# Half of the 128-row chunks kept in reverse order, so that two chunks share one left operand in the level products of a recurrent (HGRN2) branch

## The chip, the cores and the metric

The kernel runs on one core of a Trainium2 chip. The metric is the device time of one execution in microseconds (us); the median of several runs is given. The core has a matrix engine (TensorE, PE; its loads of the left operand are shown apart as PEld), VectorE (DVE), ScalarE (ACT), GpSimd (POOL), and SyncE (SP), which here only issues DMAs. The engines run side by side and wait for one another through semaphores. On-chip memory has 128 partitions; TensorE writes to a separate accumulator memory, PSUM, of which the kernel uses eight banks of 128 x 512 fp32 in three rings (`pj` 3, `z` 2, `ms` 3).

## The reference

A decoder block in fp32 over 1024 rows of width 1024: a norm, one projection to nine parts, two branches side by side, a gated sum of both, an output projection with a residual, and a dense SwiGLU FFN.

```python
xn = rms_norm(x, norm1_g); proj = xn @ w_in
q_sb, k_sb, v_sb, q_hg, f_hg, i_hg, g_hg, gate_sb, gate_hg = split_cols(proj, IN_SIZES)
# attention branch, 8 heads of 64: strictly causal stick-breaking
z = q @ k.T * scale; causal = s_idx < t_idx
sp = where(causal, softplus(z), 0); rest = cumsum(sp, reverse=True) - sp
w = where(causal, exp(log_sigmoid(z) - rest), 0); o = w @ v
# HGRN2 branch, 4 heads of 128, in order of the rows t
f = lb + (1 - lb) * sigmoid(f_hg); key = 1 - f; q = silu(q_hg)
S_t = diag(f_t) @ S_{t-1} + key_t * i_t^T;  o_t = S_t^T @ q_t
o = rms_norm(o, norm_g) * silu(g_hg)
# merge and FFN
h = x + (sigmoid(gate_sb) * (o_sb @ Wb0) + sigmoid(gate_hg) * (o_hg @ Wb1)) @ w_out
out = h + (silu(hn @ w_gate) * (hn @ w_up)) @ w_down          # hn = rms_norm(h, norm2_g)
```

In the HGRN2 branch a chunk of rows is solved at once: with b the running sum of log f over the chunk, row t gets from row s <= t the weight sum over k of q[t,k] key[s,k] exp(b[t,k] - b[s,k]).

## The kernel before, in words

All tensors lie transposed: channels in the partitions, rows (time) along the free axis. The 1024 rows are two halves (`h`) of 512, a half is four chunks of 128 rows. The x tensor comes in once, is split into a high and a low fp32r part, and stays on chip; each of the 44 column tiles of the input projection is 2 x 24 fp32r matmuls (`proj`, names `pj<-ah,oh`, `pj<-al,oh`, `pj<-ah,ol`).

The first part of the kernel (until about 700 us) holds the projections, the attention (`scores`, `values`) and the recurrent branch (`hgrn`). Operations aren't issued in program order: `Plan` collects them with their buffers and a guessed duration (`us`), and `issue()` lists them per engine: it steps through a guessed time and gives each engine the ready operation of the highest rank and, among those, of the longest remaining path. The order on each engine is thus fixed when the kernel is built, and it changes when a guessed duration changes. The projections have rank -1: TensorE takes them where nothing else is ready. Their own order is fixed by `FILL` (q, k, v as `a`, the HGRN2 parts `f`, `i`, `q`, `g`, the branch gates `G`). When the last operation of the first part is done, the pools are closed, the outputs of both branches, which were stored in DRAM (`o_d`), are loaded again (`ld`) and split (`o`), and the products with `w_branch` begin (`pj<-o,..`, `z<-o,..`).

The change lies around `hgrn`. For each head `hd` and half `h` it computes `key`, the running sums `bb` (one scan a chunk), and the 128 x 128 weights `at` of each chunk (keys in the partitions, queries along the free axis). The diagonal is a column sum (`sums`). The rest is done by levels m = 64, 32, ..., 1: in blocks of 2m rows, queries of the late half meet keys of the early half, and both are scaled against the running sum at the border, so that no exponent is positive:

- two differences on VectorE into `dl` (early keys, late queries), one Exp on ScalarE over the 512 columns, a product with `q` into `ql` and a product with `key` in `dl`;
- a matmul per chunk into `lv`: left operand `dl` of the chunk, without its last m columns, moving operand the 64 late queries of the chunk;
- the result goes to `at`, at m = 64 by a copy, below by a predicated copy with a mask of the level (`level_masks`, built on GpSimd and spread by VectorE at the start).

At m = 1 a column sum takes the place of the matmul. After the levels come the decays to the end of the chunk (`kd`, `bl`), the chunk states (`state`), the output and its norm and gate. `take` moves a projection out of PSUM: for q and k through `qk_in`, for v into `vx`. In `scores` the tile on the diagonal is masked with `future`. `setup` makes the constants. `sums`, `V`, `A`, `M`, `G` all record at one helper, so most rows of the profile have line 194 and are told apart by tile names.

Of the kernel before, what the change touches and what calls it, by code (L numbers as in the profile page):

```python
# [12 lines left out]
I8 = mybir.dt.int8  # L13
# [24 lines left out]


class View:  # L40

# [13 lines left out]
    def bitcast(self, d):  # L55
        return self._then(lambda t: t.bitcast(d))

    def to_broadcast(self, s):
# [156 lines left out]
def hybrid_block(ctx: ExitStack, tc, xT, wi, wb, wo, wg, wu, wd, vec, outT):  # L215
# [49 lines left out]
    bones_r = const1.tile([P, P], F32R, name="bones_r")  # L265
    future = const1.tile([P, P], I8, name="future")
    never = const1.tile([P, P], F32, name="never")
# [11 lines left out]
    def setup(sp):  # L279
        make_identity(nc, ident)  # L280
        t2 = sp.tile([P, P], F32, tag="t2", name="t2")
        nc.vector.memset(t2, 0.0)
        nc.vector.memset(t2[0:64, 0:64], 1.0)
        nc.vector.memset(t2[64:128, 64:128], 1.0)
        nc.vector.tensor_copy(bones_r, t2)
        nc.vector.memset(never, NEG)
        nc.gpsimd.memset(future, 1.0)
        nc.gpsimd.affine_select(
            out=future, in_=future, pattern=[[1, P]], compare_op=ALU.is_ge, fill=0.0,
            base=0, channel_multiplier=-1)  # L290
# [19 lines left out]
    def hs(h):  # L310
        return slice(h * HALF, (h + 1) * HALF)
# [56 lines left out]
    future = future.bitcast(U8)  # L368

# [9 lines left out]
        att: dict(aa=10, th=2, tl=2, ww=7, ot=2, pvt=1),  # L379
        hgp: dict(xf=2, xq=2, xi=2, xg=2, kb=4, dl=2, tail=4, ql=2,  # L380
                  state=5, bl=2),
# [111 lines left out]
    def level_masks():  # L493
        for m in LEVELS[1:]:
            mk = const1.tile([P, 4, 64], I8, name=f"mk{m}")
            one = new("tmp").bitcast(I8)[:, :64].rearrange("p (n m) -> p n m", m=m)
            G(nc.gpsimd.memset, one, 1.0, us=0.1, after=(last_split[0],))
            G(nc.gpsimd.affine_select, out=one, in_=one, pattern=[[-2 * m, 64 // m], [0, m]],
              compare_op=ALU.is_ge, fill=0.0, base=0, channel_multiplier=1, us=0.4)
            G(nc.gpsimd.affine_select, out=one, in_=one, pattern=[[2 * m, 64 // m], [0, m]],  # L500
              compare_op=ALU.is_ge, fill=0.0, base=m - 1, channel_multiplier=-1, us=0.4)
            mask = fixed(mk)
            V(nc.vector.tensor_copy, mask,
              one.rearrange("p n m -> p (n m)").rearrange("p (o t) -> p o t", o=1)
              .to_broadcast([P, 4, 64]), n=128)
            lvl_mask.append(mask.bitcast(U8))

# [79 lines left out]

    def qk_in(ps, g, h):
        x, sq = new("aa"), new("aa")
        V(tt, x, ps, rr[h], op=ALU.mult)  # L590
# [14 lines left out]
    def take(nm, u, h, ps):  # L605

        d = heads[u] if nm != "G" else None
        if nm in ("q", "k"):
            x = qk_in(ps, gains[nm], h)
            for e in range(2):  # L610
# [117 lines left out]
    def hgrn(hd, last):  # L728
# [3 lines left out]
        cs = [slice(c * P, (c + 1) * P) for c in range(4)]  # L732
        chunk = lambda t: t.rearrange("p (c t) -> p c t", t=P)
        for h in range(2):
# [4 lines left out]
            for c in cs:  # L739
                V(nc.vector.tensor_tensor_scan, bb[:, c], lf[:, c], lf[:, c], 0.0, op0=ALU.add,  # L740
                  op1=ALU.min, n=P)
            pair = lambda t, m: t.rearrange("p (n u m) -> p n u m", u=2, m=m)
            V(tt, at, key, q, op=ALU.mult, after=(last,))
# [4 lines left out]
            for li, m in enumerate(LEVELS):  # L748
                nb = HALF // (2 * m)
                bv = pair(bb, m)  # L750
                if m == 1:
                    e1 = new("ql", (P, HALF // 2))
                    ev = e1.rearrange("p (n m) -> p n m", m=1)
                    V(tt, ev, bv[:, :, 1, :], bv[:, :, 0, :], op=ALU.subtract, n=256)
                    A(act, e1, e1, AF.Exp, n=256)
                    for t, u in ((key, 0), (q, 1)):
                        V(tt, ev, ev, pair(t, 1)[:, :, u, :], op=ALU.mult, n=256)
                    lv = new("ms")
                    last = sums(lv[:, :256], e1, ones_r, 256, (last,))
                    V(nc.vector.copy_predicated, pair(at, 1)[:, :, 1, :],  # L760
                      lvl_mask[li - 1].rearrange("p c (n m) -> p (c n) m", m=1),
                      lv[:, :256].rearrange("p (n m) -> p n m", m=1), n=256)
                    continue
                rb = bv[:, :, 0, m - 1:m].to_broadcast([P, nb, m])
                dl, ql = new("dl"), new("ql", (P, HALF // 2))
                dv = pair(dl, m)
                V(tt, dv[:, :, 0, :], rb, bv[:, :, 0, :], op=ALU.subtract, n=256)
                V(tt, dv[:, :, 1, :], bv[:, :, 1, :], rb, op=ALU.subtract, n=256, part=True)
                A(act, dl, dl, AF.Exp)
                V(tt, ql.rearrange("p (n m) -> p n m", m=m), pair(q, m)[:, :, 1, :], dv[:, :, 1, :],  # L770
                  op=ALU.mult, n=256)
                V(tt, dv[:, :, 0, :], dv[:, :, 0, :], pair(key, m)[:, :, 0, :], op=ALU.mult, n=256)
                lv = new("ms")
                n = P - m
                last = M(0, [(lv[:n, c * 64:(c + 1) * 64], dl[:, c * P:c * P + n],
                                         ql[:, c * 64:(c + 1) * 64], True, True)
                                        for c in range(4)], after=(last,),
                         us=0.43 + 0.003 * n)
                dst, src = pair(at, m)[:n, :, 1, :], lv[:n, :256].rearrange("p (n m) -> p n m", m=m)
                if m == 64:  # L780
                    V(nc.vector.tensor_copy, dst, src, n=256)
                else:
                    V(nc.vector.copy_predicated, dst,
                      lvl_mask[li - 1][:n].rearrange("p c (n m) -> p (c n) m", m=m), src, n=256)
            kd, ktok, qe, bl = new("tail"), new("tail"), new("tail"), new("bl", (P, 4))
            b3 = chunk(bb)
            V(tt, chunk(kd), b3[:, :, P - 1:P].to_broadcast([P, 4, P]), b3, op=ALU.subtract,
              holds=(ktok, qe, bl))
            A(act, kd, kd, AF.Exp)
# [5 lines left out]
            d["free hq", h] = V(tt, qe, qe, q, op=ALU.mult)  # L795
            A(act, bl, b3[:, :, P - 1], AF.Exp, n=4)
            ds_ = new("ms")
# [389 lines left out]


def _layout(inputs):
    import numpy as np  # L1190

    def tiles(w):
# [12 lines left out]
    return {  # L1205
        "xT": np.ascontiguousarray(g["x"][0].T).reshape(KT, P, S),
        "wi": tiles(g["w_in"]), "wb": tiles(g["w_branch"]), "wo": tiles(g["w_out"]),
# [27 lines left out]
```

## Time and profile before

| | us |
|---|---|
| median of 3 runs (1519.15 to 1520.98) | 1520.84 |
| the profiled execution | 1520.8 |
| its span, first to last instruction | 1519.1 |
| busy: PE / DVE / ACT / POOL | 1501.8 / 1194.1 / 804.3 / 110.3 |
| level products on PE, 6 x 64 records: busy by the profile | 5.4, 6.7, 7.4, 7.7, 7.9, 8.0 |

A row such as `312.55 0.96 PE L194 MATMUL ms<-ql,dl 128*120 128x64 f32 x8` of the timeline says: at 312.55 us, lasting 0.96 us, TensorE, line 194, output `ms` from moving operand `ql` and left operand `dl`, left operand 128 partitions by 120 columns, 128 x 64 read, eight records. An fp32 matmul is two records, one of fp32r is one. In the list of groups, `x8 | 5.8, 723 | 2.1 <-PE ms` is count, busy us, mean ns of one, idle us ahead of them and what ended it. In the table of stretches each engine has its busy us and its count, then come the granted TensorE clock, the DMA share and GB/s. The ends of matmul records are modelled, and successive ones overlap.

### The profile page before, as it was taken

Reading aid. Unit: us, or ns where it says so; the run is one execution under the profiler, and the core shown is the slowest. Engines: PE = TensorE matmul, PEld = TensorE weight load, DVE = VectorE, ACT = ScalarE, POOL = GpSimd, SP = SyncE. Lnnn points to the kernel's source line nnn. Section 1 sums busy time; section 2 is a strip of 40 time slices with the busy share of each in tenths; the row PEclk is TensorE's granted clock in tenths of the full one; section 3 lists DMA queues with packets and bytes.
Section 4 is the critical chain, followed back from the end, with each engine's and each line's share of the span. In section 5 each row is a group of like instructions: output and inputs, shape, how many; then the busy total and the mean of one; then the engine's idle time right before and its main releaser. Section 6 shows DMA issues by size and latency. Waiting matters only on the chain.

```text
span 1519.1 us, 20504 instructions
## 1 busy us (share of the span) xinstructions
PE 1501.8 (99%) x7213; PEld 1238.3 (82%) x7213; DVE 1194.1 (79%) x2092; ACT 804.3 (53%) x1505; POOL 110.3 (7%) x155
## 2 busy tenths in 40 slices
PE   9999999999999999999999999999999999999999
PEld 6778888888888888888888888777888887888887
DVE  9898789988997877967867798788888888675553
ACT  7867779668758877445434453332332332354442
POOL 4210111211101100110000000000000000000000
PEclk9999999999999999999999999999999999999999
DMA  5111111111111212136434345444445544797662
GB/s 182 40 44 60 54 39 46 44 39 56 51 51 39 68 61 63 51 120 220 163 114 145 112 148 184 150 154 153 163 166 164 161 160 166 256 327 243 199 216 91
DMA packets 83159, 188.53 MB, mean 124 GB/s; under 512 B 9584, under 2 KB 11632, under 8 KB 83056
## 3 DMA queue, kind: packets, MB, share of 16 engines
q1 hardware_dynamic: 72400, 167.82, 34.2%
q10 hardware_dynamic: 10656, 19.40, 3.5%
q8 instruction: 57, 0.93, 0.3%
q14 instruction: 46, 0.38, 0.1%
HBM read 131.61 MB, written 55.57 MB: 123 GB/s over the span
## 4 chain that ended last, share of the span: by engine, by line
PE 69%; DVE 18%; DMA 5%; ACT 4%; issue 3%; POOL 1%; SPq 0%; DVEq 0%; ACTq 0%; POOLq 0%
PE pj L194 34%; PE f L1152 14%; PE ms L194 13%; PE z L194 8%; DVE ol L194 4%; DMA w<-wu 3%; DVE g L194 3%; DMA w<-wg 2%; DVE w L194 2%; DVE c L194 1%; DVE aa L194 1%; ACT aa L194 1%; ACT oh L194 1%; DVE kb L194 1%; DVE bs L194 1%
## 5 line engine op out<-in xcount | busy, mean ns | idle before, releaser
L194 PE MATMUL pj<-ah,oh 128*128 128x512 f32 x704 | 287.2, 408 | 2.4 <-ACT tmp L194 0.9
L194 PE MATMUL pj<-ah,ol 128*128 128x512 f32 x704 | 276.3, 393 | 0.0
L194 PE MATMUL pj<-al,oh 128*128 128x512 f32 x704 | 275.9, 392 | 0.0
L194 ACT CAST oh<-w 128x512 fp32r<-128x512 f32 x164 | 99.6, 619 | 237.3 <-DVE w L194 67.7
L194 DVE TENSOR_TENSOR ol<-w,oh 128x512 fp32r<-128x512 f32 x248 | 170.1, 686 | 31.0 <-ACT oh L194 23.5
L194 PE MATMUL ms<-f,oh 128*128 128x512 f32 x528 | 165.0, 394 | 3.1 <-DVE g L194 2.9
L194 PEld LDWEIGHTS pj<-ah,ol 128*128 128x128 f32 x704 | 132.6, 188 | 29.8
L194 PEld LDWEIGHTS pj<-ah,oh 128*128 128x128 f32 x704 | 132.9, 189 | 26.7 <-DVE aa L194 1.4
L194 PEld LDWEIGHTS pj<-al,oh 128*128 128x128 f32 x704 | 133.1, 189 | 23.1 <-DVE al L194 0.5
L194 PEld LDWEIGHTS ms<-f,oh 128*128 128x128 f32 x528 | 97.5, 188 | 29.5 <-DVE g L194 7.2
L1152 PE MATMUL f<-bh,ah 128*128 128x512 f32 x296 | 115.2, 389 | 0.0
L1152 PE MATMUL f<-bh,al 128*128 128x512 f32 x296 | 115.2, 389 | 0.0
L1152 PE MATMUL f<-bl,ah 128*128 128x512 f32 x296 | 115.1, 389 | 0.0
L194 DVE TENSOR_TENSOR_SCAN aa<-aa,ww 128x512 f32<-128x512 f32 (+3 forms) x96 | 94.2, 996 | 25.3 <-ACT aa L194 14.6
L194 PE MATMUL z<-f,oh 128*128 128x512 f32 x352 | 108.6, 390 | 0.0
L194 PE MATMUL pj<-f,oh 128*128 128x512 f32 x352 | 108.4, 389 | 0.0
L248 DVE TENSOR_TENSOR al<-ra,ah 128x512 fp32r<-128x512 f32 x73 | 50.4, 690 | 70.1 <-ACT ah L247 69.9
L194 PE MATMUL ms<-f,ol 128*128 128x512 f32 x264 | 102.9, 390 | 0.0
L194 POOL TENSOR_SCALAR oh<-w 128x512 fp32r<-128x512 f32 x84 | 68.4, 815 | 437.8 <-PE pj L194 367.7
L247 ACT CAST ah<-ra 128x512 fp32r<-128x512 f32 x73 | 45.5, 624 | 95.6 <-PE f L1152 83.8
L194 PE MATMUL pj<-mx,oh 128*128 128x512 f32 x256 | 78.7, 389 | 0.0
L194 PEld LDWEIGHTS pj<-f,oh 128*128 128x128 f32 x352 | 66.1, 188 | 13.7
(257 smaller groups left out, 3148.7 us busy)
## 6 DMA issues: line engine op xcount, KB each, us to landing
w<-wi SPq DMA_DIRECT2D x42, 512.0 KB, 3.6
rb<-act_d SPq DMA_DIRECT2D x73, 256.0 KB, 4.3
w<-wg SPq DMA_DIRECT2D x22, 512.0 KB, 4.3
w<-wu SPq DMA_DIRECT2D x22, 512.0 KB, 4.5
w<-wd SPq DMA_DIRECT2D x22, 512.0 KB, 5.0
wd_d<-ds SPq DMA_DIRECT2D x44, 256.0 KB, 2.8
ra<-wd_d SPq DMA_DIRECT2D x44, 256.0 KB, 4.1
act_d<-c SPq DMA_DIRECT2D x40, 256.0 KB, 4.2
```

The lines of the kernel that those rows point to most:

```text
L194: fn(*[a.real() if isinstance(a, View) else a for a in args], **{k: v.real() if isinstance(v, View) else v for k, v in kw.items()})
L247: pin(nc.scalar.copy(hi, src))
L248: pin(nc.vector.tensor_tensor(lo, src, hi.bitcast(F32), op=ALU.subtract))
L1152: nc.tensor.matmul(banks[SET[o]][d], l[:, ws], r, start=start and i == 0, stop=p == NP - 1 and i == 2, skip_group_check=True)
```

## The change

The rows of x are permuted on the host (`_order`): in each half, chunks 2 and 3 are kept in reverse order, chunks 0 and 1 in order. The output is put back on the host. Inside:

- `hgrn` scans the reversed chunks backwards. In a reversed chunk the early keys lie where a chunk in order has its late queries; `mixed` writes the early keys of chunk a (in order) and of chunk a + 2 (reversed) into one tile of 128 columns, interleaved by blocks of m. `packed` puts the late queries side by side into the second half of `dl` (the tile `ql` is gone). One matmul then has these 128 columns as left operand and 2 x 64 queries, of both chunks, as moving operand: two matmuls a level in place of four, with all 128 columns. Half of each result is meaningless and is left out by the mask.
- All levels, 64 too, now write with a predicated copy. There are seven masks, each with a form for either order, built over 128 columns and spread by four copies.
- Attention keeps queries in the stored order, and needs keys and values in true order: `ordered` takes k and v out of PSUM in two operations, the second one reversing its chunks. The diagonal mask has two forms.
- The planner's guess for a level product goes from 0.43 + 0.003 n (n = 128 - m) to 0.44 us.

```diff
@@ setup
-        nc.gpsimd.memset(future, 1.0)
-        nc.gpsimd.affine_select(out=future, ..., base=0, channel_multiplier=-1)
+        for f, base, step in ((future[0], 0, -1), (future[1], 1 - P, 1)):
+            nc.gpsimd.memset(f, 1.0)
+            nc.gpsimd.affine_select(out=f, in_=f, ..., base=base, channel_multiplier=step)
@@ level_masks
-        for m in LEVELS[1:]:
-            mk = const1.tile([P, 4, 64], I8, name=f"mk{m}")
-            one = new("tmp").bitcast(I8)[:, :64]...
+        for m in LEVELS:
+            mk = const1.tile([P, 2, 2, 64], I8, name=f"mk{m}")
+            one = new("tmp").bitcast(I8)[:, :P]...
...
-            V(nc.vector.tensor_copy, mask, one....to_broadcast([P, 4, 64]), n=128)
+            for e in range(2):
+                src = one.rearrange("p (n e) m -> p e n m", e=2)[:, e]
+                for a in range(2):
+                    V(nc.vector.tensor_copy, mask[:, e, a]..., src, n=64, part=True)
@@ qk_in (keys), take (v)
+    def ordered(x, ps, h):
+        V(tt, x[:, :256], ps[:, :256], rr[h][:, :256], op=ALU.mult, n=256, part=True)
+        chunk = lambda t: t.rearrange("p (a t) -> p a t", t=P)
+        V(tt, chunk(x[:, 256:])[:, :, ::-1], chunk(ps[:, 256:]), chunk(rr[h][:, 256:]), op=ALU.mult,
+          n=256, part=True)
-            V(tt, d["v"][:, hs(h)], ps, rr[h], op=ALU.mult, part=True)
+            ordered(d["v"][:, hs(h)], ps, h)
@@ scores
-                        V(nc.vector.copy_predicated, z[:, w - P:w], future, never, n=P)
+                        V(nc.vector.copy_predicated, z[:, w - P:w], future[tb // 2 % 2], never, n=P)
@@ hgrn
+        early = lambda t, m: t.strided(0, (256 + m, 2), (2 * m, P // m), (1, m))
+        late = lambda t, m: t.strided(m, (256 - m, 2), (2 * m, P // m), (1, m))
+        edge = lambda t, m: t.strided(m - 1, (257, 2), (2 * m, P // m), (0, m))
+        mixed = lambda t, m: t.strided(0, (m, 2), (2 * m, P // m), (1, m))
+        packed = lambda t, m, k=0: t.strided(k, (P, 2), (m, P // m), (1, m))
...
+            for i, c in enumerate(cs):
+                to, lc = (t[:, c] if i < 2 else t[:, c][:, ::-1] for t in (bb, lf))
+                V(nc.vector.tensor_tensor_scan, to, lc, lc, 0.0, op0=ALU.add, op1=ALU.min, n=P)
...
-                V(tt, dv[:, :, 0, :], rb, bv[:, :, 0, :], op=ALU.subtract, n=256)
-                V(tt, dv[:, :, 1, :], bv[:, :, 1, :], rb, op=ALU.subtract, n=256, part=True)
+                    dk, dq, rb = mixed(dl, m), packed(dl, m, 256), edge(bb, m)
+                    V(tt, dk, rb, early(bb, m), op=ALU.subtract, n=256)
+                    V(tt, dq, late(bb, m), rb, op=ALU.subtract, n=256, part=True)
                 A(act, dl, dl, AF.Exp)
...
-                last = M(0, [(lv[:n, c * 64:(c + 1) * 64], dl[:, c * P:c * P + n],
-                              ql[:, c * 64:(c + 1) * 64], True, True) for c in range(4)],
-                         after=(last,), us=0.43 + 0.003 * n)
+                    cols = lambda t, k: t.strided(k, (P, 2), (1, 64))
+                    last = M(0, [(cols(lv, 64 * a), dl[:, a * P:a * P + P],
+                                  cols(dl, 256 + 64 * a), True, True) for a in range(2)],
+                             after=(last,), us=0.44)
...
+                V(nc.vector.copy_predicated, late(at, m), packed(lvl_mask[li], m), packed(lv, m),
+                  n=256)
@@ _layout, kernel (host)
+    o = np.arange(S).reshape(S // HALF, 4, P)
+    o[:, 2:] = o[:, 2:, ::-1].copy()
```

More of the change, by code (lines that the diff above doesn't have):

```diff
@@ L37, with strided @@
 V_W = 27
+def strided(t, offset, *dims):
+    t = t[:]
+    return bass.AP(t.tensor, t.offset + offset, [t.ap[0], *(list(d) for d in dims)])
 class View:
@@ L56, in bitcast, with strided @@
         return self._then(lambda t: t.bitcast(d))
+    def strided(self, offset, *dims):
+        return self._then(lambda t: strided(t, offset, *dims))
     def to_broadcast(self, s):
@@ L265, in hybrid_block @@
     bones_r = const1.tile([P, P], F32R, name="bones_r")
-    future = const1.tile([P, P], I8, name="future")
+    future = [const1.tile([P, P], I8, name=f"future{i}") for i in range(2)]
     never = const1.tile([P, P], F32, name="never")
@@ L286, in setup @@
         nc.vector.memset(never, NEG)
-        nc.gpsimd.memset(future, 1.0)
-        nc.gpsimd.affine_select(
-            out=future, in_=future, pattern=[[1, P]], compare_op=ALU.is_ge, fill=0.0,
-            base=0, channel_multiplier=-1)
+        for f, base, step in ((future[0], 0, -1), (future[1], 1 - P, 1)):
+            nc.gpsimd.memset(f, 1.0)
+            nc.gpsimd.affine_select(out=f, in_=f, pattern=[[1, P]], compare_op=ALU.is_ge, fill=0.0,
+                                    base=base, channel_multiplier=step)
         nc.vector.tensor_scalar(qg, vt[:, V_Q:V_Q + 1], 0.125, None, op0=ALU.mult)
@@ L366, in hybrid_block @@
                          stop=i == WARM - 1)
-    future = future.bitcast(U8)
+    future = [f.bitcast(U8) for f in future]
     plan = Plan()
@@ L379, in hybrid_block @@
         att: dict(aa=10, th=2, tl=2, ww=7, ot=2, pvt=1),
-        hgp: dict(xf=2, xq=2, xi=2, xg=2, kb=4, dl=2, tail=4, ql=2,
+        hgp: dict(xf=2, xq=2, xi=2, xg=2, kb=4, dl=2, tail=4,
                   state=5, bl=2),
@@ L493, in level_masks @@
     def level_masks():
-        for m in LEVELS[1:]:
-            mk = const1.tile([P, 4, 64], I8, name=f"mk{m}")
-            one = new("tmp").bitcast(I8)[:, :64].rearrange("p (n m) -> p n m", m=m)
+        for m in LEVELS:
+            mk = const1.tile([P, 2, 2, 64], I8, name=f"mk{m}")
+            one = new("tmp").bitcast(I8)[:, :P].rearrange("p (n m) -> p n m", m=m)
             G(nc.gpsimd.memset, one, 1.0, us=0.1, after=(last_split[0],))
-            G(nc.gpsimd.affine_select, out=one, in_=one, pattern=[[-2 * m, 64 // m], [0, m]],
+            G(nc.gpsimd.affine_select, out=one, in_=one, pattern=[[-m, P // m], [0, m]],
               compare_op=ALU.is_ge, fill=0.0, base=0, channel_multiplier=1, us=0.4)
-            G(nc.gpsimd.affine_select, out=one, in_=one, pattern=[[2 * m, 64 // m], [0, m]],
+            G(nc.gpsimd.affine_select, out=one, in_=one, pattern=[[m, P // m], [0, m]],
               compare_op=ALU.is_ge, fill=0.0, base=m - 1, channel_multiplier=-1, us=0.4)
             mask = fixed(mk)
[L503 to L506, printed above, removed]
+            for e in range(2):
+                src = one.rearrange("p (n e) m -> p e n m", e=2)[:, e]
+                for a in range(2):
+                    V(nc.vector.tensor_copy, mask[:, e, a].rearrange("p (n m) -> p n m", m=m), src,
+                      n=64, part=True)
+            lvl_mask.append(mask.bitcast(U8).rearrange("p e a t -> p (e a t)"))
     xh = [[fixed(xn[k][0]) for h in range(2)] for k in range(KT)]
@@ L586, in sums, with qk_in @@
         return M(2 * n, [(out, w, hi, True, False), (out, w, lo, False, True)], after=after)
-    def qk_in(ps, g, h):
+    def ordered(x, ps, h):
[3 more added lines that the diff above has]
+          n=256, part=True)
+    def qk_in(ps, g, h, keys):
         x, sq = new("aa"), new("aa")
-        V(tt, x, ps, rr[h], op=ALU.mult)
+        if keys:
+            ordered(x, ps, h)
+        else:
+            V(tt, x, ps, rr[h], op=ALU.mult)
         A(act, sq, x, AF.Square)
@@ L733, in hgrn @@
         chunk = lambda t: t.rearrange("p (c t) -> p c t", t=P)
+        early = lambda t, m: t.strided(0, (256 + m, 2), (2 * m, P // m), (1, m))
[3 more added lines that the diff above has]
+        packed = lambda t, m, k=0: t.strided(k, (P, 2), (m, P // m), (1, m))
+        four = lambda t: t.rearrange("p (e a t) -> p e a t", e=2, a=2)
         for h in range(2):
@@ L748, in hgrn @@
             for li, m in enumerate(LEVELS):
-                nb = HALF // (2 * m)
-                bv = pair(bb, m)
+                dl, lv = new("dl"), new("ms")
                 if m == 1:
[L752 to L763, printed above, removed]
@@ L772, in hgrn @@
-                V(tt, dv[:, :, 0, :], dv[:, :, 0, :], pair(key, m)[:, :, 0, :], op=ALU.mult, n=256)
-                lv = new("ms")
-                n = P - m
-                last = M(0, [(lv[:n, c * 64:(c + 1) * 64], dl[:, c * P:c * P + n],
[L776 to L779, printed above, removed]
@@ L780, in hgrn @@
-                if m == 64:
-                    V(nc.vector.tensor_copy, dst, src, n=256)
-                else:
-                    V(nc.vector.copy_predicated, dst,
-                      lvl_mask[li - 1][:n].rearrange("p c (n m) -> p (c n) m", m=m), src, n=256)
+                    ev = packed(dl, 1)
+                    V(tt, ev, late(bb, 1), early(bb, 1), op=ALU.subtract, n=256)
+                    A(act, dl[:, :256], dl[:, :256], AF.Exp, n=256)
+                    for t in (early(key, 1), late(q, 1)):
+                        V(tt, ev, ev, t, op=ALU.mult, n=256)
@@ new lines, in hgrn @@
+                    last = sums(lv[:, :256], dl[:, :256], ones_r, 256, (last,))
+                else:
+                    dk, dq, rb = mixed(dl, m), packed(dl, m, 256), edge(bb, m)
+                    V(tt, dk, rb, early(bb, m), op=ALU.subtract, n=256)
+                    V(tt, dq, late(bb, m), rb, op=ALU.subtract, n=256, part=True)
+                    A(act, dl, dl, AF.Exp)
+                    V(tt, dq, late(q, m), dq, op=ALU.mult, n=256)
+                    V(tt, dk, dk, early(key, m), op=ALU.mult, n=256)
+                    cols = lambda t, k: t.strided(k, (P, 2), (1, 64))
+                    last = M(0, [(cols(lv, 64 * a), dl[:, a * P:a * P + P],
+                                  cols(dl, 256 + 64 * a), True, True) for a in range(2)],
+                             after=(last,), us=0.44)
@@ L785, in hgrn @@
+                V(nc.vector.copy_predicated, late(at, m), packed(lvl_mask[li], m), packed(lv, m),
+                  n=256)
             kd, ktok, qe, bl = new("tail"), new("tail"), new("tail"), new("bl", (P, 4))
-            b3 = chunk(bb)
-            V(tt, chunk(kd), b3[:, :, P - 1:P].to_broadcast([P, 4, P]), b3, op=ALU.subtract,
-              holds=(ktok, qe, bl))
+            V(tt, four(kd), bb.strided(P - 1, (P + 1, 2), (P, 2), (0, P)), four(bb),
+              op=ALU.subtract, holds=(ktok, qe, bl))
@@ L795, in hgrn @@
             d["free hq", h] = V(tt, qe, qe, q, op=ALU.mult)
[L796 removed]
+            A(act, bl.rearrange("p (e a) -> p e a", a=2), bb.strided(P - 1, (P + 1, 2), (P, 2)),
+              AF.Exp, n=4)
             ds_ = new("ms")
@@ L1186, in hybrid_block, with _order @@
         finish(o, d)
+def _order():
+    import numpy as np
+    o = np.arange(S).reshape(S // HALF, 4, P)
+    o[:, 2:] = o[:, 2:, ::-1].copy()
+    return o.reshape(S)
 def _layout(inputs):
@@ L1232 @@
     r = run_bass_kernel_spmd(nc, [arrays], core_ids=[0])
-    out = np.asarray(r.results[0]["outT"]).reshape(D, S)
+    out = np.asarray(r.results[0]["outT"]).reshape(D, S)[:, _order()]
     return np.ascontiguousarray(out.T).reshape(1, S, D)
```

14 lines of the change are left out of this document (2 added, 12 removed).

## The prediction

> **What bounds the kernel now.** I read the page first (busy shares, the chain that ended last), then the busy time by stretches, then TensorE's timeline inside the stretches that the change touches. The first 700 us of the span hold the input projections, the attention and the recurrent (HGRN2) branch; all that is edited lies there.
>
> ```profile
> span 1519.1 us, 20504 instructions
> PE 1501.8 (99%) x7213; PEld 1238.3 (82%) x7213; DVE 1194.1 (79%) x2092; ACT 804.3 (53%) x1505; POOL 110.3 (7%) x155
> PE 69%; DVE 18%; DMA 5%; ACT 4%; issue 3%; POOL 1%; SPq 0%; DVEq 0%; ACTq 0%; POOLq 0%
> ```
>
> TensorE is busy 99% and carries 69% of the chain that ended last. The ends of its records are modelled, so I don't take busy for full; I price its work by the distance from one start to the next. VectorE is the runner-up. The stretches of the level products, and the whole part from 45 to 700 us (columns: PE, PEld, DVE, ACT, POOL busy):
>
> ```profile
> 45.00:700.00 655.00, 648.67 (x3513) 544.08 (x3512) 550.17 (x1041) 473.04 (x956) 90.12 (x116) 1.00 0.20 62
> 88.00:136.00 48.00, 46.69 (x274) 39.04 (x275) 45.12 (x103) 29.32 (x58) 5.19 (x6) 1.00 0.15 48
> 256.00:322.00 66.00, 64.01 (x370) 53.80 (x369) 61.13 (x133) 41.60 (x81) 13.84 (x15) 1.00 0.14 44
> 405.00:440.00 35.00, 34.16 (x197) 27.98 (x197) 34.40 (x80) 16.84 (x32) 5.97 (x9) 1.00 0.19 63
> 614.00:660.00 46.00, 45.74 (x274) 38.72 (x273) 43.91 (x109) 19.22 (x35) 9.82 (x10) 1.00 0.19 59
> ```
>
> Over the whole part TensorE idles 6.3 us of 655 and VectorE 105 us. Inside the four level stretches (195 us) VectorE is busy 184.6, so it has only 10.4 us to spare there. TensorE never lacks work because the projections (rank -1, `pj<-ah,..`) fill each hole; a saving on TensorE therefore shortens the part as long as projections remain to be moved up.
>
> **The level products on TensorE (the gain).** Per half of a head there are six product groups, m = 64 to 2. Before, a group is four fp32 matmuls with 128-m left columns and 64 moving ones, and each fp32 matmul is two records: x8. After, it is two matmuls with 128 left and 128 moving columns: x4. One group of each width, with the start of what follows it:
>
> ```profile
> 643.47 0.68 PE L194 MATMUL ms<-ql,dl 128*64 128x64 f32 x8
> 644.07 0.50 PE L194 MATMUL pj<-ah,oh 128*128 128x512 f32 x1
> 644.88 0.81 PE L194 MATMUL ms<-ql,dl 128*96 128x64 f32 x8
> 645.50 0.47 PE L194 MATMUL pj<-ah,oh 128*128 128x512 f32 x1
> 648.81 0.95 PE L194 MATMUL ms<-ql,dl 128*112 128x64 f32 x8
> 649.59 1.11 PE L194 MATMUL ms<-xi,tail 128*128 128x128 f32 x8
> 312.55 0.96 PE L194 MATMUL ms<-ql,dl 128*120 128x64 f32 x8
> 313.31 0.47 PE L194 MATMUL ms<-th,bones_r 128*128 128x512 f32 x1
> 655.50 0.98 PE L194 MATMUL ms<-ql,dl 128*124 128x64 f32 x8
> 656.29 0.48 PE L194 MATMUL pj<-ah,oh 128*128 128x512 f32 x1
> 657.77 0.99 PE L194 MATMUL ms<-ql,dl 128*126 128x64 f32 x8
> 658.57 0.36 PE L194 MATMUL ms<-th,ones_r 128*128 128x256 f32 x1
> 306.38 0.60 PE L194 MATMUL ms<-ident,tail 128*128 128x128 f32 x4
> 306.74 0.48 PE L194 MATMUL pj<-ah,oh 128*128 128x512 f32 x1
> 654.16 0.39 PE L194 MATMUL ms<-tail,state 128*128 128x128 f32 x2
> 654.39 0.39 PE L194 MATMUL ms<-kb,xi 128*128 128x128 f32 x2
> ```
>
> The six groups take 0.60, 0.62, 0.78, 0.76, 0.79 and 0.80 us to the next start: 4.35 us per half. The moving columns are the same in all six, and yet the wide ones are a third longer: the loading of the left operand sets the pace. The new group is four records of 128 left and 128 moving columns. The nearest rows of that shape: four transposes, 0.36 us to the next start, and one fp32 matmul (two records) 654.16 to 654.39, 0.23 us. I take 0.37; 2 x 0.23 = 0.46 is the other end. Six groups: 2.22 us (2.76 at most). Eight halves: 8 x (4.35 - 2.22) = 17.0 us off TensorE (12.7 at least). The step of about 0.09 us that the first fp32r matmul behind a group costs (644.07 to 644.41 instead of 0.23) stays.
>
> [...]
>
> **VectorE.** Operation counts of a level stay: two differences, two products, one write of the result; they take half a tile each, as before. What is added:
>
> ```profile
> 667.71 0.68 DVE L194 TENSOR_TENSOR xg<-pj,rr 128x512 f32<-128x512 f32 x1
> 668.30 0.68 DVE L194 TENSOR_TENSOR ol<-w,oh 128x512 fp32r<-128x512 f32 x1
> 645.08 0.75 DVE L194 TENSOR_TENSOR dl<-kb 128x256 f32<-128x256 f32 x2
> 645.75 0.41 DVE L194 TENSOR_TENSOR ql<-kb 128x256 f32<-128x256 f32 x1
> L194 DVE COPY mk<-tmp 128x256 int8<-128x256 int8 x6 | 1.6, 283 | 0.6 <-POOL tmp L194 0.6
> L194 DVE COPY_PREDICATED kb<-mk,ms 126x256 f32<-126x256 uint8 x8 | 5.8, 723 | 2.1 <-PE ms L194 2.1
> L194 DVE COPY_PREDICATED kb<-mk,ms 96x256 f32<-96x256 uint8 x8 | 3.5, 437 | 0.0
> L194 DVE COPY kb<-ms 64x256 f32<-64x256 f32 x8 | 3.3, 408 | 0.0
> ```
>
> - k and v are taken out of PSUM in two pieces: 8 + 8 halves. One piece of 512 takes 0.59 us to the next start, two of 256 take 0.67: +0.08 x 16 = 1.3 us.
> - Masks: 6 copies of 256 bytes (1.6 us in all, 0.27 each) become 28 of 64 bytes. Between 0.07 (a quarter of that, nothing fixed) and 0.27 each: 1.9 to 7.6 us. I take 0.13, nearer the quarter, since 256 and 512 elements above (0.335 and 0.59 us) leave about 0.08 that doesn't shrink: 3.6, so +2.0 us, all in the first 45 us.
> - m = 64 becomes a predicated copy: 437 for 408 ns, x8, +0.2 us. Predicated copies at m = 2 and 1 keep their runs and their 0.72 us.
>
> Sum +3.5 us on an engine with 105 us free from 45 to 700 us. Ranges of the scan and of the last-column decay only change direction or step; I cost them at nothing, bounded by the same instruction counts.
>
> **GpSimd and start.** One more mask level, affine selects over 128 instead of 64 columns, a second causal mask:
>
> ```profile
> L194 POOL TENSOR_SCALAR_AFFINE_SELECT tmp<-tmp 128x64 int8<-128x64 int8 x12 | 7.6, 640 | 0.6
> 8.30 0.62 POOL L194 TENSOR_SCALAR oh<-kb 128x512 fp32r<-128x512 f32 x1 [4.47 <-DMA kb<-wi]
> 0.00:40.00 40.00, 36.94 (x137) 27.69 (x137) 36.37 (x71) 31.22 (x53) 16.63 (x34) 1.00 0.52 185
> ```
>
> The second causal mask (a fill and a select, 1.3 us at most by the row of the selects) comes ahead of a 4.47 us wait for a DMA: hidden. The selects of the levels: 14, each between 0.64 (the 64-wide row) and 1.28 us (twice that): 9.0 to 17.9 us against 7.6. I take 1.0: +6 us on an engine that is busy 16.6 of the first 40. The weight splits `oh` queue behind them, and VectorE's split behind those, then the projection. VectorE is busy 36.4 of those 40 us, so its +2.0 us and a late split are not fully covered: I charge 1.0 us, with 0 and 4 as ends (+2.0 and a delay of two selects).
>
> **What is late next.** In the level stretches TensorE loses 4.3 us of work per head; projections move up, and each brings VectorE about 1.2 us (an eviction, a weight split) per 5.45 us of matmuls (24 x 0.227): some 3.8 us into 10.4 us of room, but the third stretch has only 0.6. I charge 1.5 us. No DMA is moved past another: the order of loads and stores in SP's queue stays, each only earlier. The end of the part:
>
> ```profile
> 674.20 0.33 SPq L194 DMA_DIRECT2D o_d<-tail  x1
> 695.66 2.35 DVE L194 TENSOR_TENSOR o<-ld,o 128x1024 fp32r<-128x1024 f32 x2
> 700.49 0.62 PE L194 MATMUL pj<-o,oh 128*128 128x512 f32 x2
> 703.21 0.62 PE L194 MATMUL z<-o,oh 128*128 128x512 f32 x2
> ```
>
> The last store goes out at 674.2; the stored outputs come back and are split until 698.0; TensorE covers this with leftover gate projections until 700.5. The last split is wanted about 4.7 us after that start (its product is the last of the `z` group), so there are about 7 us of slack. If VectorE holds the last head's chain (614 to 660) at its length, 4.3 us of this go, and it still fits. Without that cover the overrun would be paid one to one.
>
> **Sum.** 17.0 - 1.0 - 1.5 = 14.5 us. The profiled execution took 1520.8 us around its span of 1519.1; the median of the runs is 1520.84, so the sum stands on both alike: 1506.3 us. From 700 us on nothing is edited.
>
> **Rivals.**
> - *VectorE takes the stretches.* The new patterns have one more step, and the differences and products of the left operand write interleaved. If an interleaved write cost what short runs cost the predicated copy (723 against 437 ns, 1.65 times), 96 instructions at 0.335 us would take 0.22 more: +21 us where 10.4 are free. Some 6 to 11 us of the gain go (6 if half of those 21 us find room outside the stretches), depending on how many projections can move out: about 1512. Against it: all the plain differences of a level, runs of 64 down to 2, have one row, 417 ns mean for 96 (0.335 between starts), so run length did not matter there.
> - *Nothing gained.* TensorE is paced by moving columns after all, and the added 2.5 us remain: 1521 to 1523. The group rows speak against it.
> - *Slower.* The product is now written to PSUM in two runs of 64 columns with a gap; no matmul of this trace writes with one. The decisive point: the group was 0.725 us on average, so at a record step above (0.725 - 0.05) / 4 = 0.17 us instead of 0.11 the change loses. At 1.65 times (0.185 us, group 0.77) it is +2.2 us of TensorE and +2.5 us of the rest: 1525.5. [...]
>
> ```profile
> L194 DVE TENSOR_TENSOR dl<-kb 128x256 f32<-128x256 f32 x96 | 35.5, 417 | 1.7 <-PE ms L194 1.7
> ```
>
> **Numbers.** Forecast (gain of 10 us or more) 0.72; VectorE or a disturbed order takes part (3 to 10 us left) 0.15; within 3 us either way 0.07; slower 0.06. 0.2%, 3 us, is about what a measurement here tells from no change. So faster 0.87, same 0.07, slower 0.06. The range: 1502 is all 17 us and another 2 from a luckier order; 1515 takes in the least TensorE saving with all charges (12.7 - 4 - 3 = 5.7, the 3 being twice what I charge the stretches) and most of the second case.
>
> **What would show it.** TensorE's records fall by 192, to 7021: x192 of 128*128 with 128x128 in place of x384; VectorE's rise by 16 + 22 to 2130; ScalarE's stay at 1505; GpSimd's are 160. A new group is 0.36 to 0.46 us to the next start. The gate projections end near 685 instead of 700.5, and the first product on `o` follows them without a gap. I am wrong if that gap opens, if the four-record group is over 0.6 us, if `dl` differences are over 450 ns, or if TensorE waits in 88 to 136 us grow by more than 2 us.

## The result, and the profile after

The changed kernel took 1510.97 us in the median of 6 runs (1508.5 to 1513.61), the kernel before 1519.99 us beside it (6 runs, 1517.78 to 1521.62): ratio 0.9941, interval 0.993 to 0.9953, 9.0 us. The forecast was 1506.3 us. The sign and the range held; the time is 4.7 us above the forecast, the gain (9.0 instead of 14.5) 5.5 us short, and 9.0 us lie in the second case ("3 to 10 us left", chance 0.15), just short of the likeliest ("10 us or more"). The profiled execution shown here took 1508.5 us, the shortest of the six.

The page of the changed kernel, first the head, then the share of the chain that ended last:

```profile
span 1506.8 us, 20178 instructions
PE 1485.3 (99%) x7021; PEld 1221.5 (81%) x7021; DVE 1197.3 (79%) x2130; ACT 803.5 (53%) x1505; POOL 113.7 (8%) x160
PE 60%; DVE 17%; ACT 4%; DMA 4%; issue 3%; POOL 0%; SPq 0%; DVEq 0%; ACTq 0%; POOLq 0%
```

All four counts are the predicted ones (7021, 2130, 1505, 160). TensorE is still the bound (99% busy, 60% of the chain). The stretches of the level products, by the same clock times as before (columns: length, then PE, PEld, DVE, ACT, POOL busy, clock, DMA share, GB/s):

```profile
88.00:136.00 48.00, 47.40 (x250) 38.72 (x249) 47.10 (x105) 31.11 (x61) 8.08 (x10) 1.00 0.16 51
256.00:322.00 66.00, 64.97 (x331) 53.26 (x329) 65.13 (x141) 41.84 (x84) 12.54 (x16) 1.00 0.15 47
405.00:440.00 35.00, 34.34 (x184) 28.59 (x184) 33.70 (x76) 22.37 (x46) 5.51 (x6) 1.00 0.19 59
614.00:660.00 46.00, 45.21 (x264) 38.39 (x265) 43.44 (x102) 22.41 (x41) 5.53 (x8) 1.00 0.19 62
```

VectorE is busy 189.4 us of these 195 (184.6 before): the room there went from 10.4 to 5.6 us. The groups that the prediction had priced:

```profile
L203 PE MATMUL ms<-dl 128*128 128x128 f32 x192 | 29.1, 279 | 1.6 <-DVE kb L203 0.8 <-DVE dl L203 0.5 <-ACT ww L203 0.3
L203 DVE TENSOR_TENSOR dl<-kb 128x256 f32<-128x256 f32 x104 | 41.0, 439 | 2.7 <-PE ms L203 2.5
L203 DVE COPY mk<-tmp 128x64 int8<-128x64 int8 x28 | 5.5, 280 | 1.4 <-POOL tmp L203 1.4
L203 POOL TENSOR_SCALAR_AFFINE_SELECT tmp<-tmp 128x128 int8<-128x128 int8 x14 | 10.3, 747 | 0.6
```

A product group in TensorE's timeline, with what starts behind it:

```profile
614.41 0.61 PE L203 MATMUL ms<-dl 128*128 128x128 f32 x4
614.77 0.36 PE L203 MATMUL ms<-th,vv 128*128 128x256 f32 x1
```

A new group is 0.36 us to the next start in most places (0.37 predicted), 0.41 to 0.47 in most others. Taken from start to start over all 48 groups of either trace, the products hold TensorE for 36.3 us before and 19.3 us after: 17.0 us off, as predicted. The differences run at 439 ns (417 before), so the interleaved writes cost nearly nothing. TensorE's waits in 88 to 136 us are 0.6 us in all (1.3 before). None of the signs that the prediction named for being wrong is there.

**Where it went missing.** Two stretches hold no level product, but for the first group, which starts at 87 us in both kernels. Here TensorE's busy time in them, and in the second part of the first, before and then after:

```profile
6.00:88.00 82.00, 80.38 (x352) 62.76 (x352) 76.33 (x132) 66.30 (x128) 24.08 (x38) 1.00 0.27 96
45.00:88.00 43.00, 42.66 (x207) 34.40 (x205) 39.10 (x74) 34.67 (x75) 7.02 (x10) 1.00 0.13 37
660.00:700.00 40.00, 40.00 (x185) 33.34 (x185) 25.21 (x32) 22.56 (x32) 4.15 (x5) 1.00 0.68 236
```

```profile
6.00:88.00 82.00, 76.19 (x332) 58.42 (x333) 76.69 (x152) 64.12 (x124) 26.43 (x38) 1.00 0.28 95
45.00:88.00 43.00, 40.07 (x191) 32.31 (x190) 38.50 (x84) 33.40 (x71) 10.34 (x13) 1.00 0.12 37
660.00:700.00 40.00, 38.58 (x174) 31.68 (x173) 25.01 (x32) 22.33 (x29) 3.09 (x3) 1.00 0.66 243
```

By 88 us TensorE has been busy 4.2 us less, with 20 records fewer (1.0 us was charged). Of this, 2.6 us lie in 45 to 88 us. The other 1.6 us, before 45 us, are less certain: there a run of the next section (e5), whose order up to that point is the one of before, has 36.61 us in 6 to 45 us where before has 37.72. In 45 to 88 us the two agree (42.67 and 42.66). The timelines of the changed kernel (in brackets: idle time ahead, and what ended it) show the largest piece:

```profile
47.70 1.75 DVE L203 COPY mk<-tmp 128x64 int8<-128x64 int8 x3 [1.41 <-POOL tmp L203]
...
48.23 2.40 POOL L203 TENSOR_SCALAR_AFFINE_SELECT tmp<-tmp 128x128 int8<-128x128 int8 x2
...
54.43 0.50 DVE L203 COPY_PREDICATED z<-future,never 128x128 f32<-128x128 uint8 x2
54.76 0.55 ACT L203 ACTIVATE aa<-z 128x256 f32<-128x256 f32 x2 [2.55 <-DVE z L203]
54.84 0.75 DVE L203 TENSOR_TENSOR vx<-pj,rr 128x256 f32<-128x256 f32 x2
55.40 0.68 PE L203 MATMUL ms<-ident,vx 128*128 128x128 f32 x4 [2.17 <-ACT aa L203]
```

A mask copy stands in VectorE's queue, and VectorE waits 1.41 us for GpSimd's select (0.63 us at the last mask copy before). From there it works without a break until 56.1, so everything queued behind the copy comes later, the diagonal mask (54.43) and v (54.84) among it; ScalarE and TensorE wait in turn, TensorE for 2.17 us.

At the end of the part the first product on `o` moved from 700.49 to 690.29 without a gap of its own, but a wait stands a little ahead of it:

```profile
680.53 1.23 DVE L203 TENSOR_TENSOR o<-ld,o 128x1024 fp32r<-128x1024 f32 x1 [1.61 <-ACT o L203]
681.67 0.69 DVE L203 TENSOR_TENSOR ol<-w,oh 128x512 fp32r<-128x512 f32 x1
682.41 0.50 PE L203 MATMUL pj<-ah,ol 128*128 128x512 f32 x1 [1.42 <-DVE ol L203]
...
690.29 0.61 PE L203 MATMUL pj<-o,oh 128*128 128x512 f32 x2
```

VectorE waits 1.61 us for a piece of `o`, and the weight split of a gate projection is queued behind it.

So in the profiled executions: 17.0 - 4.2 - 1.4 leaves 11.4; measured are 10.2 up to the first product on `o`; a remainder of 1.2 us lies elsewhere. The prediction charged 1.5 us to the level stretches, but that the remainder lies there isn't shown: by the tables TensorE idles 3.1 of their 195 us, and 4.4 before. (A wait shorter than a record's modelled end doesn't show as idle time: the row of 614.41 ends at 615.02, 0.25 us behind the next start.) Behind the first product on `o` nothing is edited, and 818.6 us became 816.5; in eleven of the twelve runs below it is 814.4 to 819.2, in the twelfth (e10) 824.1. This account is by place only. What causes each part is for the experiments, and they agree with it only in part.

### The profile page after: what moved, and what is told of

It is laid out like the page before. It is cut to its first block, busy times and chain, and to the rows that moved or that the text cites. A ratio compares the mean times of both kernels' runs of the same rounds, so it can differ in the third digit from the quotient of the medians.

```text
span 1506.8 us, 20178 instructions
## 1 busy us (share of the span) xinstructions
PE 1485.3 (99%) x7021; PEld 1221.5 (81%) x7021; DVE 1197.3 (79%) x2130; ACT 803.5 (53%) x1505; POOL 113.7 (8%) x160
## 4 chain that ended last, share of the span: by engine, by line
PE 60%; DVE 17%; ACT 4%; DMA 4%; issue 3%; POOL 0%; SPq 0%; DVEq 0%; ACTq 0%; POOLq 0%
PE pj L203 26%; PE f L1170 14%; PE ms L203 11%; PE z L203 9%; DVE ol L203 4%; DVE g L203 2%; DVE dl L203 2%; DMA w<-wu 2%; DMA w<-wg 2%; DVE kb L203 1%; DVE aa L203 1%; DVE w L203 1%; ACT aa L203 1%; DVE c L203 1%; DVE tl L203 1%
```

## The experiments

The theories. A: the mask work at the start took the missing gain. B: VectorE holds part of the level stretches, so that TensorE's time there passes on only in part. C: the order of the kernel before was an unusually good one. D: every edit redraws the planner's order, and this moves the time by itself.

**The products alone, with the order held.** First the kernel before with only the planner's guess for a level product set to 0.44, as in the changed kernel. Then the same with the products as two matmuls of 128 moving columns (left width n as before). This second kernel multiplies the second chunk of each pair by the first one's left operand, so half of its level products are of the wrong keys; it stands for the time alone. Both have the same operations in the same order on each engine.

```diff
- us=0.43 + 0.003 * n)          # four matmuls, n left x 64 moving columns
+ us=0.44)                      # e5: the guess only
+ ... for c in range(2)], after=(last,), us=0.44)   # e1: two matmuls, n left x 128 moving
```

> The kernel before, with the planner's guess for a level product at 0.44 us as in the changed kernel, and the old four matmuls: no work is changed, only the order on the engines. Theory C, formed from the first four runs (products alone gain 11 us and not 14 to 17; masks alone and two pieces alone each cost 3 to 4 us, far over their work): the order of the kernel before is an unusually good one, and any other order costs 2 to 4 us, whatever the edit: 1522 to 1525. Theory A (the masks' waits are the loss): as before, 1519 to 1521. Theory B (VectorE holds the stretches): as before, 1519 to 1521.

> The kernel before, with its level products alone in the new shape: two matmuls with 128-m left and 128 moving columns in place of four with 64 (the second chunk of each pair is multiplied by the first one's left operand, so half of the level products are of the wrong keys); masks, key and value pieces, order of rows and differences as before. Theory A (the saving on TensorE passes to the end almost whole; what the change lost, it lost in the first 60 us to the masks and the two-piece evictions): 14 to 17 us less than before, 1503 to 1506. Theory B (VectorE holds the level stretches, so part of the saving can't pass, whatever the masks do): the same 7 to 11 us as the whole change, 1509 to 1513. First product on o in the trace: A near 684 to 687 us, B near 690.

Measured: guess alone 1517.18 us (ratio 0.9986, 0.9977 to 0.9996), faster than any theory expected; with the new products 1509.54 us (0.9927, 0.9914 to 0.994). Between the two, 0.9927 / 0.9986 = 0.9941 or 9.0 us, and the first product on `o` moves from 699.10 to 689.38, 9.7 us. The cause of the gain is thus shown: it is the shape of the products. A group moves 256 columns in both kernels, 4 x 64 and 2 x 128, so the rival "nothing gained" (TensorE paced by moving columns) would have no gain between these two; this pair rules it out here, but for the groups with 64 left columns (0.61 and 0.58 us, below).

With the order held, the two traces can be compared record by record. From start to start the products take 20.6 us instead of 35.0, so 14.4 us come off TensorE, and not 17: the eight groups of m = 64, which keep their 64 left columns here, take 0.58 us each, hardly less than the 0.61 of the four matmuls. All other records together lose 4.7 us: 1.5 in 88 to 136 us, 2.2 in 256 to 322 us, 0.4 before 45 us, 0.6 in all other places. So two thirds of what TensorE saves pass on to the first product on `o` (9.7 of 14.4). In 256 to 322 us TensorE waits 0.9 us for VectorE with the new products and has no such wait without them, which fits B.

The 1.5 us in 88 to 136 us are the clock's (granted 0.96 there with the new products, 1.00 in the guess alone). One and the same wait stands in both, here in TensorE's timeline of the guess alone:

```profile
114.56 0.50 PE L194 MATMUL pj<-ah,oh 128*128 128x512 f32 x1 [2.19 <-ACT tmp L194]
114.89 0.40 PE L194 MATMUL pj<-al,oh 128*128 128x512 f32 x1
115.13 0.39 PE L194 MATMUL pj<-ah,ol 128*128 128x512 f32 x1
```

and with the new products:

```profile
113.39 0.79 PE L194 MATMUL pj<-ah,oh 128*128 128x512 f32 x1 [2.38 <-ACT tmp L194]
113.98 0.63 PE L194 MATMUL pj<-al,oh 128*128 128x512 f32 x1
114.41 0.63 PE L194 MATMUL pj<-ah,ol 128*128 128x512 f32 x1
...
116.90 0.40 PE L194 MATMUL pj<-ah,oh 128*128 128x512 f32 x1
```

Its stretch (the granted clock, 0.96, is the third number from the end):

```profile
88.00:136.00 48.00, 45.62 (x236) 37.20 (x235) 43.63 (x99) 29.32 (x56) 6.72 (x8) 0.96 0.16 53
```

After 2.19 us of idling the steps stay at 0.23 us; after 2.38 us they are 0.43 until 116.9, eight matmuls, some 1.5 us lost. It isn't the longer wait that decides. The wait of 2.17 us ahead of `ms<-ident,vx` stands in the changed kernel and in e12 (below), first without and then with slow steps behind it (granted clock 1.00 and 0.96 in 45 to 88 us):

```profile
56.16 0.39 PE L203 MATMUL pj<-al,oh 128*128 128x512 f32 x1
56.39 0.40 PE L203 MATMUL pj<-ah,ol 128*128 128x512 f32 x1
```

```profile
55.89 1.09 PE L203 MATMUL ms<-ident,vx 128*128 128x128 f32 x4 [2.17 <-ACT aa L203]
...
57.20 0.63 PE L203 MATMUL pj<-al,oh 128*128 128x512 f32 x1
57.63 0.63 PE L203 MATMUL pj<-ah,ol 128*128 128x512 f32 x1
```

**The other parts alone.** The kernel before with the new mask building (seven levels, 28 copies), and with k and v taken out of PSUM in two pieces:

```diff
+ for e in range(2):
+     for a in range(2): V(nc.vector.tensor_copy, mask[:, e, a]..., src, n=64, part=True)    # e2
+ for s in (slice(0, 256), slice(256, 512)): V(tt, x[:, s], ps[:, s], rr[h][:, s], ...)      # e3
```

> The kernel before, with the masks built in the new way and nothing else: seven levels over 128 columns on GpSimd and 28 copies of 64 bytes on VectorE (all four with the mask of chunks in order, that of m = 64 unused). A: VectorE's mask copies wait for selects that take longer than planned, and what is queued behind them is late: 3 to 5 us more than before, 1523 to 1525, lost before 65 us of the span. B: no change within 1 us, 1519 to 1521.

> The kernel before, with k and v taken out of PSUM in two operations of 256 columns in place of one of 512, both in order. 16 more VectorE operations, 0.08 us each: A: 0 to 1 us more, 1520 to 1521. B: 1 to 2 us more, since VectorE has no room in the level stretches.

Measured: masks 1523.71 us (1.0023, 1.0012 to 1.0034), as A expected; two pieces 1524.36 us (1.0026, 1.0015 to 1.0037), more than either theory did. The stretches of the masks alone:

```profile
6.00:88.00 82.00, 77.02 (x332) 58.59 (x332) 76.46 (x149) 63.60 (x124) 25.27 (x40) 1.00 0.28 96
45.00:88.00 43.00, 41.36 (x192) 32.98 (x192) 38.62 (x85) 33.46 (x73) 11.45 (x17) 1.00 0.12 37
```

TensorE is busy 3.4 us less than before up to 88 us (4.2 in the changed kernel), 1.3 of it from 45 us on. That the masks cost time at the start is what A says. But the parts don't add up: -11.1 (products and guess) + 3.5 + 4.0 is -3.6, and the change as a whole gives -9.0. Something else moves with each edit.

**The order alone.** The guessed time of the transposes in the kernel before (e6), and the same edit in the changed kernel (e11); true guesses for GpSimd's mask work in the changed kernel (e4). Not one operation changes.

```diff
- plan.op("P", 0.11 * len(outs) - 0.08, [(nc.tensor.transpose, ...   # e6, e11
+ plan.op("P", 0.12 * len(outs) - 0.08, [(nc.tensor.transpose, ...
- memset us=0.1, affine_select us=0.4                                # e4
+ memset us=0.2, affine_select us=0.9
```

> The kernel before, with the planner's guess for a transpose at 0.12 instead of 0.11 us and nothing else: the same instructions in another order. C: 2 to 4 us more than before, 1522 to 1525. A and B: 1519 to 1521.

> The changed kernel with the guessed time of transposes changed, the same instructions in another order. D (order alone moves -2 to +8 us): 1509 to 1519, and still faster than the kernel before, which lost 8 us to the same edit (1527.33). If the changed kernel's order is an unlucky one: 1507 or less.

> The changed kernel, with the planner's guess for the mask work on GpSimd near what the trace shows: 0.2 us for the fill (was 0.1) and 0.9 us for a select (was 0.4). The work is the same, only the order on the engines changes. A: the mask copies are no longer listed ahead of their masks, VectorE doesn't wait, 2 to 4 us of the loss come back: 1507 to 1509. B: no change, 1510 to 1512.

Measured: e6 1527.33 us (1.0052, 1.0035 to 1.0069), slower than any theory expected; e11 1514.0 us (0.9962, 0.9948 to 0.9977), within D's range; e4 1510.36 us (0.9936, 0.9919 to 0.9954), where A had expected 2 to 4 us off. So D is shown: the same operations in another order are 8 us slower in the kernel before, 2 us faster with the guess of e5 (against C: the order of before isn't the best), 3 us slower in the changed kernel, and the same with e4. In e6 a single wait stands out, in the list of TensorE's waits from 440 to 500 us (total, times, longest):

```profile
PE z L194 <- DVE ww L194: 3.9, 1, 3.9
```

and with it a lowered clock (0.97) in the stretch:

```profile
450.00:500.00 50.00, 45.91 (x238) 38.43 (x237) 37.83 (x65) 37.49 (x79) 10.05 (x11) 0.97 0.15 46
```

From e6 to e11, the whole change under one and the same other guess, the gain is 13.6 us (0.9962 / 1.0052), near the forecast of 14.5. From e5 to e1 it was 9.0 for the products alone, in the kernels as given 9.0. One other order makes 4 to 5 us of difference in what the change is worth.

**The products twice.** The changed kernel with each level product issued twice, with the guess doubled (e7), and with the guess left, so that all else keeps its order (e12):

```diff
- ... for a in range(2)], after=(last,), us=0.44)
+ ... for a in (0, 1, 0, 1)], after=(last,), us=0.88)   # e7
+ ... for a in (0, 1, 0, 1)], after=(last,), us=0.44)   # e12
```

> The changed kernel with each level product issued twice (four matmuls a group with 128 left and 128 moving columns, guess 0.88 us): 192 records more at about 0.112 us, 21.5 us of TensorE. A and C: all of it passes to the end, 19 to 24 us more than the changed kernel, 1530 to 1535 (C allows 3 us either way for the order). B: part of it hides in time in which TensorE waits for VectorE in the level stretches: 10 to 16 us more, 1521 to 1527.

> The changed kernel with each level product issued twice on TensorE and its guess left, so that the order of all else is that of the changed kernel. 48 more groups of 0.37 to 0.45 us: 17 to 22 us of TensorE work. If TensorE alone sets the part up to the first product on o, that start moves by all of it: 17 to 22 later, 1528 to 1533. B (VectorE holds part of the level stretches, so that TensorE's work there passes only in part): 11 to 15 later, 1522 to 1526.

Measured: e7 1525.78 us (1.005, 1.0032 to 1.0068), e12 1524.84 us (1.0039, 1.0025 to 1.0052). A doubled group in e12:

```profile
629.33 1.05 PE L203 MATMUL ms<-dl 128*128 128x128 f32 x8
630.14 0.48 PE L203 MATMUL pj<-ah,oh 128*128 128x512 f32 x1
...
707.12 0.61 PE L203 MATMUL pj<-o,oh 128*128 128x512 f32 x2
```

0.81 us for 0.36. Over all groups, start to start, it is 40.0 us instead of 19.3, so 20.7 us of work. The first product on `o` comes 16.8 us later (17.5 in e7), the time rises by 0.0098 of 1520, 14.9 us (16.6). So 0.7 to 0.8 of TensorE time that is added passes on; by the time this is B's number, by the start it ends at the edge between the two. Record by record, e12 having the order of the changed kernel, the added work takes the place of 3.9 us that TensorE spent otherwise, and 4.2 us of that saving lie in the four level stretches (0.3 are lost elsewhere). In the same four stretches VectorE is now busy 178.8 us of 195 (189.4 in the changed kernel). So in the changed kernel TensorE does lose some 4 us to other engines in these stretches, which fits B. How much of this came with the change isn't shown: no run doubles the products of the kernel before.

**The masks later.** In the changed kernel the masks built behind the weight split of the first head's last input projection, moved only (e9); moved, with 14 copies of 128 bytes and GpSimd's true guesses (e8); the latter with the other guess for transposes (e10).

```diff
-            level_masks()                 # at i == 0
+            if i == 5:                    # behind the weight split of the first head's last input
+                level_masks()
- for a in range(2): V(nc.vector.tensor_copy, mask[:, e, a]..., n=64)      # e8, e10 only
+ V(nc.vector.tensor_copy, mask...(two chunks), one...(read twice), n=128)
```

> The changed kernel with the masks built later (behind the weight split of the projection hi of the first head instead of at the start), 14 copies of 128 bytes in place of 28 of 64, and the guess for the selects at 0.9 us. A: the first 60 us lose no more than before: 3 to 4 us better than the changed kernel, 1507 to 1508. B: no change, 1510 to 1512. C: another order, 1508 to 1513.

> The changed kernel with one edit: the level masks are built behind the weight split of the first head's last input projection instead of ahead of the first; 28 copies of 64 bytes and the old guesses stay. A (the mask work at the start is where the missing gain went: TensorE lost 3 us of it in 45 to 65 us): 1505 to 1508, like the kernel with late masks (1505.87), and the first product on o at 686 to 688. Rival (it was the halved number of copies, or the luck of the order): no faster than the changed kernel by more than 1 us, 1510 to 1513.

> The kernel with late masks (1505.87) with the guessed time of transposes changed, so that the planner gives another order of the same instructions. If the late masks carry their gain by themselves: faster than the same edit on the changed kernel by 3 to 5 us (run beside it). If it was luck of the order: equal to that one within 1 us. D (order alone moves -2 to +8 us): somewhere in 1504 to 1514.

Measured: e8 1505.87 us (0.9906, 0.9891 to 0.9921), faster than both kernels and than any theory expected; e9 1517.89 us (0.9982, 0.9971 to 0.9994), 10 us off what A expected and above its rival too; e10 1525.56 us (1.0038, 1.0025 to 1.0051), above all that was expected. The stretches, of e8:

```profile
45.00:88.00 43.00, 42.45 (x209) 34.94 (x209) 37.85 (x76) 38.29 (x83) 10.46 (x22) 1.00 0.12 39
```

of e9:

```profile
45.00:88.00 43.00, 42.46 (x209) 35.00 (x209) 38.05 (x82) 38.76 (x84) 11.08 (x22) 1.00 0.12 39
136.00:200.00 64.00, 60.80 (x331) 51.83 (x331) 52.33 (x103) 42.60 (x80) 7.48 (x12) 0.95 0.18 55
```

and of e10, with TensorE's timeline below them:

```profile
45.00:88.00 43.00, 42.37 (x206) 34.53 (x205) 38.72 (x76) 36.72 (x81) 13.43 (x23) 1.00 0.13 38
88.00:136.00 48.00, 38.81 (x195) 32.33 (x195) 45.27 (x110) 29.41 (x60) 8.74 (x12) 0.86 0.11 36
```

```profile
94.44 0.68 PE L203 MATMUL ms<-dl 128*128 128x128 f32 x4 [1.81 <-DVE kb L203]
96.63 1.19 PE L203 MATMUL ms<-dl 128*128 128x128 f32 x4 [1.50 <-DVE kb L203]
...
104.60 1.20 PE L203 MATMUL ms<-dl 128*128 128x128 f32 x4 [3.96 <-DVE kb L203]
```

In all three, 2.3 to 2.4 of the 2.6 us that were lost in 45 to 88 us come back: that cost of the masks is real. (Before 45 us e8 and e9 have 36.14 and 36.03 us, as the changed kernel has 36.12, so the loss there isn't shown to be the masks'.) But e9 and e10 lose more behind it. In e10 no projection stands among the product groups from 92 to 105 us. TensorE waits for other engines ahead of each, for VectorE above all, on which the late mask copies now stand in between (about 0.14 us each); the granted clock falls to 0.50 in 96 to 108 us (a product group takes 1.19 instead of 0.68 by its row), and 9 of 48 us are idle. So A falls as the account of the net: taking the mask work off the start is worth 2 to 3 us there, and what it does to the whole is decided by the order that comes of it. The gain of e8 isn't shown to be its edit's; it is one order, the best of those tried.

## Why the prediction was right or wrong

Right in sign and range, and in what the products' shape saves TensorE (17.0 us); 4.7 us too far in the time, 5.5 in the gain.

| step | predicted | measured |
|---|---|---|
| level products on TensorE | 34.8 to 17.8, 17.0 off, group 0.37 | 36.3 to 19.3, 17.0 off, group 0.36 mostly, 0.40 on average |
| start | 1.0 on (0 to 4) | TensorE 4.2 less busy by 88 us, 2.6 of it from 45 us on |
| VectorE: masks | +2.0 busy | 5.5 - 1.6 = +3.9 busy |
| GpSimd: selects | +6 busy | 10.3 - 7.6 = +2.7 busy |
| end of the part | 0 | a wait of 1.42 |
| level stretches | 1.5 on | not to be told apart in a remainder of 1.2; with the order held 4.1 of 14.4 saved don't pass (e1), 4.2 of 20.7 added don't (e12) |
| first product on `o` | near 686 (700.5 - 14.5) | 690.29 |

- *The products.* The term came out to the tenth, in part by luck: one group of each width gave 34.8 us where all groups take 36.3, and 0.37 us a group was 0.03 under the average of the new ones, so two errors of 1.5 us cancel.
- *The failed term is the start.* It was priced by busy time and capped near the upper end, 4, by a delay of two selects. The copies were not the trouble: 23 of the 28 take 0.10 us to the next start (0.13 taken), four take 0.27 to 0.57, 4.4 us in all. A copy in VectorE's queue waited 1.41 us for GpSimd and held up what was behind it, where the prediction only asked what is queued behind the selects on GpSimd.
- *"What is late next" had the wrong place.* The slack of 7 us was right for `o` itself. What wasn't asked: earlier `o` pieces stand in VectorE's queue ahead of a weight split, and wait there.
- *The stretches.* VectorE was rightly named the runner-up, and not by the rival's mechanism (439 ns where I set 450 as a limit). But counting what is moved in against its free time, 3.8 into 10.4 us, is too kind: in the pair with the order held 4.1 of 14.4 us didn't pass in these stretches, 1.5 of it by the clock. The predicted 1.5 was neither confirmed nor refuted by the change itself.
- *The order.* It was in the second case by name and in the low end ("a luckier order", 2 us). The runs with nothing but a guess changed moved by -2 to +8 us. A term of this size belonged in the sum's range on both sides, and how the 4.7 us divide between start, stretches and order stays open, since no edit to one leaves the order of the others.
- *The rival "slower" fell*: PSUM output in two runs with a gap costs nothing that shows here. The group with the gap is 0.36 us, and with one run (e1, the rows below) 0.35. (The rival's price was mis-added: four steps of 0.185 us are 0.74 and not 0.77, which gives 1524.0 and not 1525.5.)

```profile
625.80 0.60 PE L194 MATMUL ms<-ql,dl 128*124 128x128 f32 x4
626.15 0.48 PE L194 MATMUL pj<-ah,oh 128*128 128x512 f32 x1
```

## What to carry to other kernels

Where fp32 matmuls of equal moving columns take longer the more left columns they have (0.61 us a group with 64, 0.80 with 126, in the kernel before), packing two products under one left operand can pay (36.3 us became 19.3): price it from start to start, over all groups and not over one of each kind, and expect a part of it. Two thirds to four fifths passed on here, with VectorE 92 to 95% busy in the same stretches. A small operation put into an engine's queue costs its wait (1.41 us ahead of the mask copy at 47.70; a copy behind another one takes 0.10), and this fell on all that was queued behind it, so look at its producer and not at its length. With a planner that reorders on every edit, run the same operations in two or three orders before a difference of under 10 us is given to an edit.

## What the runs showed of the hardware

- TensorE's granted clock fell after some waits of 2.2 to 2.4 us and not after others, so the length of the wait alone doesn't decide it. It fell after 2.38 us (e1, 113.39; 0.96 in 88 to 136 us) and after 2.17 us (e12, 55.89; 0.96 in 45 to 88 us), and didn't after 2.17 us (changed kernel, 55.40; 1.00 in 55.4 to 58.8 us), 2.19 us (e5, 114.56; 1.00 in 88 to 136 us) or 2.42 us (e3, in 660 to 700 us; 1.00 there). While it was low, the steps of matmuls with 512 moving columns were 0.43 us instead of 0.23; in e1 they are back at 0.23 from 116.90 on. The lowest stretch read is 96 to 108 us of e10, with 0.50.
- Fewer left columns aren't always cheaper. With 128 moving columns (e1) four records with 64 left columns take 0.58 us to the next start, and 0.35 to 0.51 us with 96 or more (one, with a wait inside, 0.90). With 64 moving columns (e5) eight records take 0.61 us with 64 left columns and 0.80 with 126. At 64 left columns two matmuls of 128 moving columns thus gained next to nothing over four of 64. That more left columns make a group longer is shown with 64 moving columns, and not with 128.
- Back to back, a copy of 128 x 64 int8 takes 0.10 us to the next start, one of 128 x 256 0.20 us (before). A select over 128 columns takes 747 ns on average where one over 64 took 640; single ones vary more than that (0.40 to 1.20 us in the changed kernel).
